# A decoder step on one core: another order of tiles on reused bytes, and four scalings on another engine

## The chip, the core and the metric

The kernel runs on one core of a Trainium2 chip. Five engines work beside each other, each through a queue of its own in order: TensorE (PE in the profile; PEld is its weight load), VectorE (DVE), ScalarE (ACT), GpSimd (POOL) and SyncE (SP), which here issues most DMA transfers. An instruction at the head of a queue that has to wait holds up all that stands behind it. The metric is the device time of one execution in microseconds; lower is better.

## The reference

One layer of a hybrid decoder, for a prompt of 512 tokens and eight samples of four new tokens each that share all weights:

```python
h = rmsnorm(x, w['norm1']) * (1 + sc1) + sh1
bg, cg, xin, q, kc, vc, ks, vs, kw, vw, nsa_g, merge_g = split_columns(h @ w['w_in'])
v, conv_new = short_conv(cg * xin, conv_prev, w['w_conv'], w['b_conv'])
y_a = (bg * v) @ w['w_out_conv']
o_b, nsa_state = attend(qh, gates, kvh(kc, vc), kvh(ks, vs), kvh(kw, vw))
y_b = o_b @ w['w_o_nsa']
x = x + g1 * ((ga * y_a + gb * y_b) @ w['w_out'])
h2 = rmsnorm(x, w['norm2']) * (1 + sc2) + sh2
x = x + g2 * ((jax.nn.silu(h2 @ w['w_gate']) * (h2 @ w['w_up'])) @ w['w_down'])
```

The attention has three branches, each with its own softmax: over compressed blocks, over selected blocks, over a window. The outputs are added with one gate for each head and branch:

```python
s_w = jnp.einsum('bqgrd,bkgd->bgrqk', q, kw).astype(jnp.float32) - sl * w_dist
p_w = jax.nn.softmax(jnp.where(w_valid, s_w, NEG), axis=-1)
o_w = jnp.einsum('bgrqk,bkgd->bqgrd', p_w.astype(vw.dtype), vw)
o = gates[..., 0:1] * o_c + gates[..., 1:2] * o_s + gates[..., 2:3] * o_w
```

The prompt attends to itself; with 512 tokens all its blocks are selected. The samples attend to 1,024 older tokens in a paged cache as well.

## The kernel before

Activations lie feature by feature: 128 partitions, eight slices of features, 544 tokens (32 of the samples, 512 of the prompt). Large products are made of three matmuls each (L247 to L249), with both operands split in a high and a low part: ScalarE copies the high part, VectorE subtracts it. The weights come as slabs of 1 MB through SyncE's queue into a ring of three buffers (L233, tile `raw`).

The stages in order: compressed keys of the samples; input projections; sample attention, in four pairs of samples, with the rest of the projections and the short convolution as filling between its steps; prompt attention; output projections; feed-forward. The change lies at the passage from sample to prompt attention.

**Sample attention** (`rows_gen`, L1116 on) keeps the cache rows in a ring of seven buffers of 8 KB per partition (`sraw`, `wraw`; pool `srp`). Each pair takes four for selected rows (two samples, two halves each) and two for window rows, in turn. For each pair TensorE computes the selected scores, multiplies the selected values (L1166 on `sraw`), then the window scores and the window values (L1166 on `wraw`). There follow a transpose of the remaining probabilities (L1187), the product of these (L1195) and a transpose of the output (L1200).

**Prompt attention** goes through four head groups `g`, and in each through four blocks of 128 queries, `i` = 3, 2, 1, 0. `cmp_probs(g)` makes the compressed probabilities: eight matmuls (L1340), a copy by ScalarE (L1342), four transposes (L1345), then VectorE's operations L1352 to L1360. `unit(g, i)` makes the scores of the two other branches (L1385, L1386, or L1378, L1379 for short blocks). VectorE adds the distance table and finds the row minimum (L1391), ScalarE takes the exponential and the row sum (L1392), VectorE scales by gate over sum (`fac`, L1401). Then TensorE transposes the probabilities (L1416), ScalarE copies them (now and then VectorE, L1333 and L1335), and TensorE multiplies the values (L1410). The eight probability tiles of the first unit, `g` = 0 and `i` = 3, use the output tile `oT` as storage. Between the pieces of the first unit, the last input projections (`for _ in fill`, L247 to L249 on `h`) and the splits of the convolution's output (`split_y`, L380 and L381 on `yin`) are made; behind it come the projections of that output (`oc_gen`) and the modulation products (`mod_slab`, L399).

**What is loaded for it** at its start, all through SyncE's queue: the table `ta` (L1281, 0.32 MB), the queries of the first group (`q_stack`, L1297), its keys, high and low (`k_stack`, L1290), the values of both branches (`vtok`, L1303) and two slabs behind them (L1305). Two tiles for queries and two sets for keys take turns by `g % 2`.

**Where these tiles lie.** The framework gives pools bytes like a stack, from two ends. The row ring is given back before prompt attention starts (`cst2.close()`), and the pool `at1` lies on its bytes. A new tile waits for the last reader of every old tile that it overlaps, and for that alone. Within a pool the tiles lie upwards in the order in which the code makes them. From the sizes (queries 8 KB per partition, high and low keys 4 KB each, values 4 KB for each branch, table 2.5 KB), `at1` begins 14,464 bytes into the ring. In the last pair the ring's seven buffers hold, from below: selected rows of the second sample, second half and first half; of the first sample, second half and first half; window rows of the pair before, no longer read; window rows of the second sample; of the first sample. So the tiles lie now:

| tile | bytes of the ring | what lay there |
|---|---|---|
| first queries `qs0` | 14,464 to 22,656 | selected rows |
| second queries `qs1` | 22,656 to 30,848 | selected rows |
| values `vtok0` | 30,848 to 34,944 | selected rows, free buffer |
| values `vtok1` | 34,944 to 39,040 | free buffer |
| second keys | 39,040 to 47,232 | free buffer, window rows |
| first keys | 47,232 to 55,424 | window rows of both samples |
| table `ta` | 55,424 to 57,984 | window rows of the first sample, and 640 bytes above the ring |

**The order of the queues.** A planner of the framework orders each engine's queue when the program is built: it takes the instructions in program order but lets a later one go ahead of one that, by its own reckoning, still waits. PSUM tiles of the tag `g` (five buffers) serve projections, transposes and half of the scores.

Of the kernel before, what the change touches and what calls it, by code (L numbers as in the profile page):

```python
# [10 lines left out]
F32 = mybir.dt.float32  # L11
F32R = mybir.dt.float32r
I32 = mybir.dt.int32
AF = mybir.ActivationFunctionType
# [7 lines left out]
TP = 512  # L22
# [125 lines left out]
TA_W = 512 + 128  # L148
# [3 lines left out]
def build(tc, a, o):  # L152
    nc = tc.nc
    sync, act, dve, pool, pe = nc.sync, nc.scalar, nc.vector, nc.gpsimd, nc.tensor
    top = ExitStack()

    def mkpool(stack, name, space=None, side="left"):
        if space is DRAM:
            return stack.enter_context(tc.tile_pool(name=name, bufs=1, space=DRAM))
        if space is PSUM:  # L160
            return stack.enter_context(tc.tile_pool(name=name, bufs=1, space=PSUM))
        return stack.enter_context(tc.tile_pool(name=name, bufs=1, side=side, reuse_waits="tile"))
# [9 lines left out]
    def tp_ps(nm):  # L172
        return ps.tile([128, 512], F32, tag="g", bufs=5, name=nm)

    def s_ps(nm):
        return ps.tile([128, 512], F32, tag="sc", bufs=2, name=nm)

    def acc_ps(nm):
        return ps.tile([128, 512], F32, tag="acc", bufs=1, name=nm)
# [3 lines left out]
    def nm(s):  # L183
        uid[0] += 1
        return f"{s}_{uid[0]}"
# [1088 lines left out]
    C = yinf  # L1274
    pst = ExitStack()
    at1 = mkpool(pst, "at1", side="right")
    qs_ = [at1.tile([128, 4, TP], F32R, name=f"qs{j}") for j in range(2)]
    vtok = [at1.tile([128, 4, 256], F32, name=f"vtok{br}") for br in range(2)]
    ks_ = [[at1.tile([128, 2, TP], F32R, name=f"k{n}{j}") for n in "hl"] for j in (1, 0)][::-1]
    ta = at1.tile([128, TA_W], F32, name="ta")  # L1280
    sync.dma_start(ta, a["tab_a"])  # L1281
    t_dist = ta[:, 0:512]
    t_cd = ta[:, 512:640].rearrange("p (i c) -> p i c", i=4)
# [46 lines left out]
    def pev(out, in_):  # L1330
        pcnt[0] += 1
        if pcnt[0] % 6:
            act.activation(out, in_, AF.Copy)  # L1333
        else:
            dve.tensor_copy(out, in_)  # L1335
# [28 lines left out]
    def unit(g, i, ks, qs, pc, beside=lambda r: None):  # L1364

        n = 128 * (i + 1)
        gp, gg = g // 2, g % 2
        sums = at.tile([128, 8], F32, tag="sums", bufs=2, name=nm("sums"))
        nms = at.tile([128, 8], F32, tag="nms", bufs=2, name=nm("nms"))
        P = {}  # L1370
        for r in range(4):
            hs = SLOPES[4 * g + r]
            ql = qs[:, r, 128 * i:128 * i + 128]
            kh, kl = ks
            if 2 * n <= 512:
                sp = s_ps(nm("sp"))[:, 0:2 * n]
                spv = sp.rearrange("p (b x) -> p b x", b=2)
                pe.matmul(sp, lhsT=ql, rhs=kh[:, :, 0:n], start=True, stop=False)  # L1378
                pe.matmul(sp, lhsT=ql, rhs=kl[:, :, 0:n], start=False, stop=True)  # L1379
                sps = [spv[:, 0, :], spv[:, 1, :]]  # L1380
            else:
                sps = []
                for br in range(2):
                    sp = (s_ps if br else lin_ps)(nm("sp"))
                    pe.matmul(sp[:, 0:n], lhsT=ql, rhs=kh[:, br, 0:n], start=True, stop=False)  # L1385
                    pe.matmul(sp[:, 0:n], lhsT=ql, rhs=kl[:, br, 0:n], start=False, stop=True)  # L1386
                    sps.append(sp[:, 0:n])
            for br in range(2):
                c = br * 4 + r
                t = oT[:, br * 4 + r, :] if g == 0 and i == 3 else atp.tile([128, 512 if i % 2 else 384], F32, tag="PX" if i % 2 else "PY", bufs=8, name=nm("P"))  # L1390
                p_ops.append(dve.tensor_tensor_reduce(out=t[:, 0:n], in0=sps[br], in1=t_dist[:, 512 - n:512], scale=-hs, scalar=3e38, op0=ALU.add, op1=ALU.min, accum_out=nms[:, c:c + 1]))  # L1391
                e_ops.append(act.activation(t[:, 0:n], t[:, 0:n], AF.Exp, scale=-1.0, bias=nms[:, c:c + 1], accum_out=sums[:, c:c + 1]))  # L1392
                P[br, r] = t
            beside(r)
        fac = at.tile([128, 8], F32, tag="fac", bufs=2, name=nm("fac"))
        dve.reciprocal(fac, sums)
        dve.tensor_mul(fac.rearrange("p (b r) -> p b r", b=2), fac.rearrange("p (b r) -> p b r", b=2), gtok[:, i, g * 12:(g + 1) * 12].rearrange("p (r b) -> p b r", b=3)[:, 1:3])
        for br in range(2):
            for r in range(4):
                c = br * 4 + r  # L1400
                dve.tensor_scalar_mul(P[br, r][:, 0:n], P[br, r][:, 0:n], fac[:, c:c + 1])  # L1401
        yield
        acc = acc_ps(nm("acc"))
        pend = None
        tp = tp_ps(nm("ctp"))
        pe.transpose(tp[:, 0:128], pc[:, i].rearrange("p r c -> p (r c)"), ident)
        act.activation(pct, tp[:, 0:128], AF.Copy)
        def pv_pair(j, pts_):
            for br in range(2):
                pe.matmul(acc[br * 64:br * 64 + 64, :], lhsT=vtok[br][:, j, g * 64:(g + 1) * 64], rhs=pts_[br], start=(j == 0), stop=False)  # L1410
        for j in range(i + 1):
            pts_ = []
            for br in range(2):
                tp = tp_ps(nm("ptp"))
                for r in range(4):
                    pe.transpose(tp[:, r * 128:(r + 1) * 128], P[br, r][:, 128 * j:128 * j + 128], ident)  # L1416
                ptt = at.tile([128, 512], F32, tag="PT", bufs=4, name=nm("PT"))
                pev(ptt, tp)
                pts_.append(ptt)
            if pend is not None:  # L1420
                pv_pair(*pend)
            pend = (j, pts_)
        pv_pair(*pend)
        for r in (0, 2, 1, 3):
            q = (r // 2) * 64
            pe.matmul(acc[q:q + 64, r * 128:(r + 1) * 128], lhsT=vm[:, g, r, :], rhs=pct, start=False, stop=(r % 2 == 1))
        tmp = at.tile([128, 512], F32, tag="PT", bufs=4, name=nm("otmp"))[0:64]
        act.activation(tmp, acc[64:128, :], AF.Copy)
        dve.tensor_add(oT[gg * 64:gg * 64 + 64, gp * 4:gp * 4 + 4, 128 * i:128 * i + 128], acc[0:64, :].rearrange("p (r q) -> p r q", r=4), tmp.rearrange("p (r q) -> p r q", r=4))
# [5 lines left out]

    first_pc = cmp_probs(0, qst)
    first_unit = unit(0, 3, kst, qst, first_pc, split_y)
    next(first_unit)
    for _ in fill:
# [18 lines left out]
    for g in range(4):  # L1458
        qs, ks = qst, kst
        pc = cmp_probs(g, qs) if g else first_pc  # L1460
        for i in (3, 2, 1, 0):
            u = unit(g, i, ks, qs, pc) if g or i < 3 else first_unit
            if g or i < 3:
                next(u)
            next(ocf, None)
            mod_slab(nslab, mods_ahead.pop(0) if mods_ahead else None)
            nslab += 1
            if prev is not None:
                next(prev, None)
            prev = u  # L1470
            if g < 3 and i == 3:
                qst = q_stack(g + 1)
            if g < 3 and i == 2:
                kst = k_stack(g + 1)
# [27 lines left out]
    for k2 in range(4):  # L1502
        sy = slab("o", k2)
        for kk in range(2):
            k = k2 * 2 + kk
# [406 lines left out]
```

## Time and profile before

| | |
|---|---|
| median of 3 runs | 1240.37 us (1239.27 to 1240.58) |
| the profiled execution | 1242.07 us, of which its span 1240.3 us |
| mean granted TensorE clock | 0.994 |
| instructions | 25,490 |
| HBM read, written | 181.60 MB, 29.11 MB |

The profile is one execution. A row of the timeline gives start, duration, engine, line, operation and tiles, and in brackets how long the engine had been idle and what released it. A row of the windows gives a stretch, its length, the busy time of each engine with the number of instructions, the granted clock, the share of the DMA engines and GB/s. A row of the waits gives who waited for what, the sum, how often, the longest. A row of one tile or line gives the shortest, median and longest duration in ns. Durations of neighbours overlap a little, since an engine starts an instruction before the one ahead has quite ended; a sequence is measured from start to start.

### The profile page before, as it was taken

To read this page: it belongs to the slowest core of one execution; us is meant where nothing else is said; L and a number is where in the kernel's file an instruction comes from. 1 tells how busy PE (TensorE), PEld (TensorE's weight loads), DVE (VectorE), ACT (ScalarE), POOL (GpSimd) and SP (SyncE) were. 2 spreads that over 40 slices of the span, in tenths; PEclk is the share of its full clock that TensorE was granted. 3 is DMA by queue.
4 is the path that set the end of the run, shared out by engine and by line. 5 is a ranking of instruction groups with operands and counts; after the bars stand their busy time and mean duration, and the time that the engine had idled before them with its cause. 6 is when DMAs were issued, how large, how long until landed. Compare 5 with 4: busy or idle time off the path is not lost.

```text
span 1240.3 us, 25490 instructions
## 1 busy us (share of the span) xinstructions
PE 1215.6 (98%) x10254; PEld 1122.1 (90%) x10254; DVE 834.6 (67%) x1853; ACT 624.6 (50%) x1206; POOL 54.3 (4%) x105
## 2 busy tenths in 40 slices
PE   8999999999999999979999999999999999999997
PEld 6999999999999888867767778999999999999997
DVE  4467427687775567666858776667985688666866
ACT  5456435564545433347667666436653255424542
POOL 1000310000000101110000000001000000000000
PEclk9999999999999999989999999999999999999999
DMA  8954244364443998594744325333532433223212
GB/s 285 408 204 168 96 157 154 131 204 157 156 147 131 342 351 296 217 254 154 213 120 138 136 87 209 106 136 101 156 137 99 161 114 136 103 103 136 86 52 73
DMA packets 58920, 205.14 MB, mean 165 GB/s; under 512 B 7208, under 2 KB 13224, under 8 KB 43578
## 3 DMA queue, kind: packets, MB, share of 16 engines
q1 hardware_dynamic: 56898, 199.57, 46.4%
q0 software_dynamic: 1472, 3.56, 1.4%
q8 instruction: 80, 1.31, 0.5%
q10 hardware_dynamic: 432, 0.39, 0.1%
q14 instruction: 38, 0.31, 0.1%
HBM read 181.60 MB, written 29.11 MB: 170 GB/s over the span
## 4 chain that ended last, share of the span: by engine, by line
PE 55%; DVE 2%; ACT 1%; DMA 1%; issue 0%; DVEq 0%; SPq 0%; ACTq 0%
PE lin L247 5%; PE lin L248 5%; PE lin L249 5%; PE wA L247 4%; PE dn L247 4%; PE dn L249 4%; PE dn L248 3%; PE acc L1410 3%; PE wA L248 3%; PE wA L249 3%; PE ptp L1416 3%; PE wC L249 2%; PE wC L248 2%; PE wC L247 2%; PE modp L399 1%; PE sp L1385 1%
## 5 line engine op out<-in xcount | busy, mean ns | idle before, releaser
L247 PE MATMUL lin<-h_h,wh 128*128 128x288 f32 (+1 forms) x416 | 122.3, 294 | 0.0
L248 PE MATMUL lin<-h_l,wh 128*128 128x288 f32 (+1 forms) x416 | 120.2, 289 | 0.0
L249 PE MATMUL lin<-h_h,wl 128*128 128x288 f32 (+1 forms) x416 | 119.7, 288 | 0.0
L242 ACT ACTIVATE wh<-raw 128x1024 fp32r<-128x1024 f32 x62 | 65.5, 1056 | 102.5 <-PE lin L248 38.2
L243 DVE TENSOR_TENSOR wl<-raw,wh 128x1024 fp32r<-128x1024 f32 x62 | 76.0, 1226 | 36.8 <-ACT wh L242 36.0
L247 PE MATMUL dn<-f_hilo,wh 128*128 128x288 f32 (+1 forms) x304 | 88.0, 290 | 0.1
L249 PE MATMUL dn<-f_hilo,wl 128*128 128x288 f32 (+1 forms) x304 | 87.6, 289 | 0.0
L248 PE MATMUL dn<-f_hilo,wh 128*128 128x288 f32 (+1 forms) x304 | 87.2, 287 | 0.0
L247 PEld LDWEIGHTS lin<-h_h,wh 128*128 128x128 f32 x416 | 79.0, 190 | 7.7 <-issue 6.9
L248 PEld LDWEIGHTS lin<-h_l,wh 128*128 128x128 f32 x416 | 78.5, 189 | 0.2
L249 PEld LDWEIGHTS lin<-h_h,wl 128*128 128x128 f32 x416 | 78.1, 188 | 0.1
L1392 ACT ACTIVATE P<-P,nms 128x384 f32<-128x384 f32 (+3 forms) x120 | 65.0, 544 | 23.8 <-DVE nms L1391 23.1
L296 ACT ACTIVATE work<-wA 128x272 f32<-128x272 f32 x111 | 43.8, 395 | 61.7 <-PE wA L249 59.9
L648 PE MATMUL phi<-xh,wph 128*128 128x256 f32 x256 | 72.0, 290 | 1.5 <-ACT xh L630 1.0
L1391 DVE CUSTOM_DVE_ANT_0 P<-sp,ta 128x384 f32<-128x384 f32 (+3 forms) x120 | 52.3, 469 | 31.4 <-PE sp L1379 24.4
L648 PE MATMUL phi<-xl,wph 128*128 128x256 f32 x256 | 70.5, 284 | 0.9 <-DVE xl L631 0.9
L648 PE MATMUL phi<-xh,wpl 128*128 128x256 f32 x256 | 70.2, 283 | 0.0
L381 DVE TENSOR_TENSOR Wl<-ws,Wh 128x1024 fp32r<-128x1024 f32 x37 | 45.3, 1225 | 32.2 <-ACT Wh L380 31.9
L380 ACT ACTIVATE wh<-raw 128x1024 fp32r<-128x1024 f32 (+2 forms) x41 | 42.2, 1030 | 31.5 <-PE dn L248 13.1
L380 ACT ACTIVATE wh<-ws 128x1024 fp32r<-128x1024 f32 x37 | 39.3, 1061 | 37.0 <-PE wB L248 23.6
L247 PEld LDWEIGHTS dn<-f_hilo,wh 128*128 128x128 f32 x304 | 57.1, 188 | 0.6 <-ACT f_hilo L380 0.3
L249 PEld LDWEIGHTS dn<-f_hilo,wl 128*128 128x128 f32 x304 | 57.3, 189 | 0.1
(506 smaller groups left out, 4125.6 us busy)
## 6 DMA issues: line engine op xcount, KB each, us to landing
raw<-in_wt SPq DMA_DIRECT2D x97, 1024.0 KB, 5.3
sraw<-in_cache_sel SPq DMA_DIRECT2D x64, 256.0 KB, 5.0
gt<-in_cache_cmp SPq DMA_DIRECT2D x56, 256.0 KB, 5.2
wraw<-in_cache_winT SPq DMA_DIRECT2D x8, 1024.0 KB, 9.5
out_new_win_sample<-in_cache_win SPq DMA_DIRECT2D x8, 512.0 KB, 5.8
out_new_win_sample<-in_cache_win SPq DMA_DIRECT2D x8, 504.0 KB
out_kvT<-kvT SPq DMA_DIRECT2D x12, 272.0 KB, 2.1
raw<-in_wt SPq DMA_DIRECT2D x4, 768.0 KB, 4.3
```

The lines of the kernel that those rows point to most:

```text
L242: act.activation(oh, view, AF.Copy)
L243: dve.tensor_sub(ol, view, oh.bitcast(F32))
L247: pe.matmul(p, lhsT=wh[:, k, :], rhs=xh, start=start, stop=False, **kw)
L248: pe.matmul(p, lhsT=wh[:, k, :], rhs=xl, start=False, stop=False, **kw)
L249: pe.matmul(p, lhsT=wl[:, k, :], rhs=xh, start=False, stop=stop, **kw)
L296: o_.snap_ops.append(act.activation(t, p, AF.Copy))
L380: act.activation(hi, src, AF.Copy)
L381: return dve.tensor_sub(lo, src, hi.bitcast(F32))
L648: pe.matmul(po[:, s * 256:s * 256 + 256], lhsT=w, rhs=m, start=(n_ == 0), stop=(n_ == len(ops) - 1))
L1391: p_ops.append(dve.tensor_tensor_reduce(out=t[:, 0:n], in0=sps[br], in1=t_dist[:, 512 - n:512], scale=-hs, scalar=3e38, op0=ALU.add, op1=A ...
L1392: e_ops.append(act.activation(t[:, 0:n], t[:, 0:n], AF.Exp, scale=-1.0, bias=nms[:, c:c + 1], accum_out=sums[:, c:c + 1]))
L1410: pe.matmul(acc[br * 64:br * 64 + 64, :], lhsT=vtok[br][:, j, g * 64:(g + 1) * 64], rhs=pts_[br], start=(j == 0), stop=False)
```

## The change

The tiles of `at1` are made in another order, and the second four of the eight scalings in the very first unit go to ScalarE.

```diff
-    qs_ = [at1.tile([128, 4, TP], F32R, name=f"qs{j}") for j in range(2)]
+    k_tiles = lambda j: [at1.tile([128, 2, TP], F32R, name=f"k{n}{j}") for n in "hl"]
+    qs_ = [at1.tile([128, 4, TP], F32R, name="qs0")]
+    ks_ = [k_tiles(0)]
+    ta = at1.tile([128, TA_W], F32, name="ta")
     vtok = [at1.tile([128, 4, 256], F32, name=f"vtok{br}") for br in range(2)]
-    ks_ = [[at1.tile([128, 2, TP], F32R, name=f"k{n}{j}") for n in "hl"] for j in (1, 0)][::-1]
-    ta = at1.tile([128, TA_W], F32, name="ta")
+    qs_.append(at1.tile([128, 4, TP], F32R, name="qs1"))
+    ks_.append(k_tiles(1))
     sync.dma_start(ta, a["tab_a"])
...
-                dve.tensor_scalar_mul(P[br, r][:, 0:n], P[br, r][:, 0:n], fac[:, c:c + 1])
+                if g == 0 and i == 3 and br:
+                    act.activation(P[br, r][:, 0:n], P[br, r][:, 0:n], AF.Copy, scale=fac[:, c:c + 1])
+                else:
+                    dve.tensor_scalar_mul(P[br, r][:, 0:n], P[br, r][:, 0:n], fac[:, c:c + 1])
```

The sizes stay, so the pool covers the same bytes. By the same arithmetic the tiles then lie:

| tile | bytes of the ring | what lay there |
|---|---|---|
| first queries `qs0` | 14,464 to 22,656 | selected rows |
| first keys | 22,656 to 30,848 | selected rows |
| table `ta` | 30,848 to 33,408 | selected rows, free buffer |
| values `vtok0` | 33,408 to 37,504 | free buffer |
| values `vtok1` | 37,504 to 41,600 | free buffer, 640 bytes of window rows |
| second queries `qs1` | 41,600 to 49,792 | window rows of both samples |
| second keys | 49,792 to 57,984 | window rows of the first sample, and 640 bytes above the ring |

The transfers and their place in the program stay as they are. The `if` holds for `g` = 0, `i` = 3 and the second branch (`br` = 1), so for four instructions of 128x512 in the whole program.

## The prediction

> **What bounds the kernel now.** I read the page first: engine shares, slices, the chain that ended last. Then who waited for whom on TensorE, then windows and the timeline of the one stretch with a long wait.
>
> ```profile
> PE 1215.6 (98%) x10254; PEld 1122.1 (90%) x10254; DVE 834.6 (67%) x1853; ACT 624.6 (50%) x1206; POOL 54.3 (4%) x105
> engine line waited for: us in total, times, longest us
> PE cpt L1340 <- DMA qs<-q_dr0l: 6.1, 1, 6.1
> ...
> PE lin L247 <- DVE nms L1391: 1.3, 1, 1.3
> ...
> PE sp L1385 <- DMA kh<-k_dr0h: 0.3, 1, 0.3
> ```
>
> TensorE is busy for 98% of the span, so time is won only where it stands still or runs slowly. In its waits over the whole run the longest is 6.1 us: the first compressed scores of the prompt's attention (L1340) wait for the query load. A wait of 1.3 for the first score sums of the second unit follows a little later. Both lie in the stretch that the change edits. What TensorE and SyncE do there:
>
> ```profile
> 511.48 1.95 PE L1166 MATMUL sacc<-sraw,pts 128*32 128x128 f32 x64
> 522.59 1.08 PE L1166 MATMUL sacc<-wraw,pts 128*32 128x128 f32 x32
> 526.27 0.33 PE L1200 MATMUL ot<-ident,ob 128*128 128x128 f32 x1 [0.40 <-ACT ob L1197]
> 532.67 1.94 PE L1340 MATMUL cpt<-qs,kcd 128*32 128x512 f32 x8 [6.07 <-DMA qs<-q_dr0l]
> 534.92 0.77 PE L1385 MATMUL sp<-kh,qs 128*128 128x512 f32 x1 [0.32 <-DMA kh<-k_dr0h]
> 535.49 1.06 PE L1345 MATMUL cps<-ident,cpT 128*128 128x128 f32 x4
> 536.20 2.48 PE L1385 MATMUL sp<-kh,qs 128*128 128x512 f32 x5
> 538.48 0.41 PE L247 MATMUL lin<-h_h,wh 128*128 128x256 f32 x1
> SPq L1281 <- PE ptx L1187: 20.9, 1, 20.9
> 501.50 1.48 SPq L233 DMA_DIRECT2D raw<-in_wt  x2
> 523.70 0.33 SPq L1281 DMA_DIRECT2D ta<-in_tab_a  x1
> 524.64 0.59 SPq L1297 DMA_DIRECT2D qs<-q_dr0l  x1
> 526.55 1.29 SPq L1290 DMA_DIRECT2D kl<-k_dr0l  x2
> 527.89 1.07 SPq L1303 DMA_DIRECT2D vtok<-v_dr  x2
> 530.28 2.65 SPq L233 DMA_DIRECT2D raw<-in_wt  x2
> 535.91 1.28 SPq L1290 DMA_DIRECT2D kh<-k_dr0h  x2
> SPq L1290 <- DMA kl<-k_dr0l: 1.0, 2, 0.6
> 513.50:523.70 10.20, 9.59 (x102) 8.15 (x94) 7.86 (x19) 3.07 (x7) 1.04 (x2) 1.00 0.01 2
> 528.00:529.00 1.00, 0.00 (x0) 0.00 (x0) 0.00 (x0) 0.00 (x0) 0.00 (x0) 0.75 1.08 246
> 532.70:538.50 5.80, 5.48 (x19) 3.16 (x20) 1.85 (x3) 0.60 (x1) 0.00 (x0) 0.50 1.04 314
> ```
>
> SyncE's queue stands for 20.9 us, from the slab loads at 501.50 to 523.70, at the table load (L1281). The table lies on the last pair's first window rows, so it may only land when TensorE has multiplied the window values (L1166 on wraw, 522.59 + 1.08 = 523.67); the profile names the transpose behind it. Queries and keys stand behind the table in that queue, and the keys lie on window rows themselves. In the 10.2 us of this standing the transfer engines move nothing (DMA share 0.01). Then everything is loaded at once, while TensorE finishes its sample work at 526.60 and has nothing until 532.67. Meanwhile its granted clock falls and stays at half through the first scores (0.50).
>
> **The change, part by part.** *The order of the tiles.* Worked out from the sizes in the code, the queries stay where they are (rows of two selected parts); the first keys move onto selected rows, the table onto selected rows and a window buffer of the pair before; the first values follow on that old buffer, the second values reach 640 bytes into the last pair's second window rows. Second queries and keys take the last pair's window rows. So table, queries and keys now wait for the selected values, 511.48 + 1.95 = 513.43, instead of 523.67. Nothing is added or removed: the same loads in the same sizes, 10.2 us earlier, into a stretch where DMA does nothing.
>
> When do they land? Before, the first scores began 8.97 us after the table's issue (523.70 to 532.67), with everything else in flight too; 513.43 + 8.97 gives 522.4. The loads of the second keys at 535.91 waited for the landing of the first low keys (the row under it), so the latter were there when the second of the two was issued, 536.55 at the latest: 12.85 after the table, so 526.3. TensorE asks for the queries at 526.60 and for the low keys one us later. Both margins are positive, 4.2 and over 1 us. The new wait that the change brings, second values on window rows, stands in SyncE's queue until 523.67; behind it are the two slabs of L1305 and the second queries and keys. Before, those slabs went at 530.28, so they go earlier as well.
>
> What TensorE gains: the idle 6.07, the wait for the keys 0.32, and the slow clock. For the last I take the same work where the clock is full, the next head group:
>
> ```profile
> 594.57 1.07 PE L1340 MATMUL cpt<-qs,kcd 128*32 128x512 f32 x8
> 595.57 0.50 PE L1385 MATMUL sp<-kh,qs 128*128 128x512 f32 x1
> 596.61 0.60 PE L1345 MATMUL cps<-ident,cpT 128*128 128x128 f32 x4
> 596.96 0.48 PE L1385 MATMUL sp<-kh,qs 128*128 128x512 f32 x1
> ```
>
> There eight compressed-score matmuls take 1.00 from start to start, four score matmuls 1.04 (0.26 each), four transposes 0.35. The first unit runs eight, six and four between 532.67 and 538.48: 1.00 + 1.56 + 0.35 = 2.91 at full clock, against 5.81 - 0.32 = 5.49 now. The slow clock costs 2.58. After the change I expect no gap over the 0.40 that stands before L1200, so none of it.
>
> [...]
>
> *Half the first scaling on ScalarE.* Of the eight scalings of the first unit (L1401) the last four leave VectorE.
>
> ```profile
> 540.46 0.69 DVE L1391 CUSTOM_DVE_ANT_0 oT<-sp,ta 128x512 f32<-128x512 f32 x1 [1.02 <-PE sp L1386]
> 553.92 4.20 DVE L1401 TENSOR_SCALAR oT<-oT,fac 128x512 f32<-128x512 f32 x7
> 555.89 1.15 DVE L1401 TENSOR_SCALAR oT<-oT,fac 128x512 f32<-128x512 f32 x2
> 558.03 0.54 DVE L1391 CUSTOM_DVE_ANT_0 P<-sp,ta 128x384 f32<-128x384 f32 x1
> 558.64 0.39 PE L247 MATMUL lin<-yin_hi,wh 128*128 128x256 f32 x1 [1.29 <-DVE nms L1391]
> 563.65 1.91 PE L1416 MATMUL ptp<-ident,oT 128*128 128x128 f32 x16
> 553.03 1.05 ACT L242 ACTIVATE wh<-raw 128x1024 fp32r<-128x1024 f32 x1
> 558.62 0.62 ACT L1392 ACTIVATE P<-P,nms 128x384 f32<-128x384 f32 x1 [3.49 <-DVE nms L1391]
> 562.83 0.60 ACT L1392 ACTIVATE P<-P,nms 128x384 f32<-128x384 f32 x1
> L907 ACT ACTIVATE qh<-work,hd x8: 723/724/727, 237.5 to 274.5; 128x512 fp32r<-128x512 f32 x8
> ```
>
> On VectorE the four take 2.14 (555.89 to 558.03). TensorE stands 1.29 until the next unit's first sum, which is queued right behind them. ScalarE idles 3.49 there, and its nearest form, a copy scaled per partition on 128x512 (L907), takes 0.72: four take 2.9.
>
> Does the 1.29 go? The softmax chain of the first unit starts at 540.46 (L1391), 1.02 of which VectorE waited for TensorE; so it was through with the compressed scores at 539.44, 3.95 after the transposes of L1345 began, 3.49 with these at full clock (0.60 for 1.06). From L1340 to L1345 it is 2.04 in the later group. So the chain starts at 526.60 + 2.04 + 3.49 = 532.1, 8.3 earlier. VectorE comes to the second unit at 558.03 - 8.3 - 2.14 = 547.6 and is done with its first sum 0.54 later, 548.1. TensorE wants that at 557.35 (558.64 less the wait) less 6.07 + 0.32 + 2.58, 548.4. So the 1.29 goes. ScalarE ends the split of L242 at 554.08 - 8.3 = 545.8, the scalings at 548.7, then the eight exponentials that now last from 558.62 to 563.43: 553.5. TensorE needs it for the transposes' copies soon after 563.65 - 10.26 = 553.4. That fits with nothing to spare, and ScalarE is late next.
>
> Sum: 6.07 + 0.32 + 2.58 + 1.29 = 10.26. I count 10.2, with 0.1 for ScalarE. From there on TensorE's own work sets the pace:
>
> ```profile
> 600.00:700.00 100.00, 100.00 (x864) 1.00 0.45 142
> ```
>
> There TensorE is 100% busy with a DMA share under one half, so what is won before is kept. The profiled execution took 1242.07 (span 1240.3 and 1.8 around it) and would take 1231.9. The median, 1240.37, lies 1.7 below it; less 10.2 it is **1230.2**.
>
> **Rivals.** *ScalarE becomes the bound* of the first two units. For: it has no slack, and the four scalings may be queued ahead of the weight split or behind the exponentials. If each takes up to the 1.05 of the 1024-column pass of L242 instead of 0.72, that is 1.3, and with a bad order up to 2: 1231.5 to 1232.2. Against: the scalings fill an idle 3.49.
>
> *The loads are not hidden, or only in part*: the planner, which orders every queue at build time, puts the second values, with their wait until 523.67, ahead of queries or keys, or they land slowly. If wholly so, only the 1.29 is won: 1239.1. Twice the landing time (18 us after 513.43) leaves a gap of 4.8 and a cold start, a gain of some 3: 1237. Against: the values' loads come last in the program and in the trace (527.89); the transfer engines are free.
>
> *Slower: the first scores move ahead in TensorE's queue.* The planner does move work past waiting work: the slab load at 501.50 stands behind the table in the program. If it believes the queries present at, say, 513.5, the eight matmuls of L1340 stop TensorE until 522.4, 9.0 us where it now loses 6.07 + 0.32, at half clock after two of them (2.6 as now), and the sample's last work follows behind: 2.6 more, 1243.0. It decides from a place in the queue before about 513.5; by 520 the stop is 2.4 and most of the gain stays. Against: the accumulators of L1340 come from the same five-buffer ring as the transposes before it, and the trace takes these in program order, L1200 first, L1340 behind.
>
> **How the numbers follow.** The forecast with its small errors (1228.5 to 1231): 0.64. ScalarE the bound (1231 to 1232.5): 0.16. Loads hidden in part or not at all (1234 to 1239.5): 0.09, half of it within 0.2%, which is 2.5 us and about what a measurement of this kernel can tell from no change. Slower (1241 to 1245): 0.05. More than forecast, because the chain starts on VectorE before the compressed scores and fills the 0.40 before L1200: 1226.5 to 1228.5, 0.06. Range 1227.5 to 1233.5, which leaves out the third and fourth case and half of the last. Faster 0.90, within 0.2% 0.05, slower 0.05.
>
> **What would show it.** Right: the table's issue near 513.5 and a DMA share well above 0.01 up to 523.7; no wait of L1340 or L1385 for a DMA; clock 1.00 through 540; the transposes of L1416 ten us earlier; ScalarE with four copies of about 0.7 on oT. Wrong: SyncE still at the table at 520, L1340 with a wait anywhere, TensorE waiting for ScalarE in L1416 or L1410, or a later stretch where it is less than 99% busy.

## The result and the profile after

| | before | after |
|---|---|---|
| median of 6 runs each | 1240.47 us (1239.27 to 1240.95) | 1231.35 us (1230.64 to 1233.15) |
| ratio, 95% interval | | 0.993 (0.9917 to 0.9942) |
| the profiled execution | 1242.07, span 1240.3 | 1232.06, span 1230.3 |
| mean granted TensorE clock | 0.994 | 0.998 |

The median fell by 9.1 us. The forecast was 1230.2, with a range of 1227.5 to 1233.5; for the profiled execution 1231.9, where 1232.06 was measured.

SyncE's queue after the change, from the timeline (start, duration, engine, line, tiles). The changed code stands three lines further down, and six lines from the scalings on.

```profile
513.17 0.33 SPq L1284 DMA_DIRECT2D ta<-in_tab_a  x1
514.04 0.51 SPq L1300 DMA_DIRECT2D qs<-q_dr0h  x1
515.24 2.34 SPq L1293 DMA_DIRECT2D kh<-k_dr0h  x2
517.63 1.24 SPq L1293 DMA_DIRECT2D kl<-k_dr0l  x2
518.91 5.72 SPq L1306 DMA_DIRECT2D vtok<-v_dr  x2
```

The table goes out at 513.17 instead of 523.70, with queries and keys right behind it. The two value loads now hold the place in which the table used to wait: 5.72 with the second one's wait for the window rows. The same stretch in the windows (length, busy time of PE, PEld, DVE, ACT and POOL, granted clock, DMA share, GB/s):

```profile
513.50:523.70 10.20, 9.60 (x108) 8.24 (x104) 8.43 (x19) 3.64 (x7) 0.47 (x1) 1.00 0.92 210
528.00:540.00 12.00, 11.71 (x81) 10.46 (x78) 10.24 (x26) 7.98 (x19) 1.72 (x2) 1.00 1.03 301
```

A DMA share of 0.92 stands where it was 0.01, and TensorE does as much in it as before (9.60 for 9.59); from the last selected value products to L1200 it takes 14.78 (512.06 to 526.84), 14.79 before (511.48 to 526.27): the loads cost the sample work nothing. In the second row the clock is 1.00 where it was 0.50 up to 538.5. TensorE in that place, timeline:

```profile
526.84 0.33 PE L1200 MATMUL ot<-ident,ob 128*128 128x128 f32 x1 [0.40 <-ACT ob L1197]
527.10 1.07 PE L1343 MATMUL cpt<-qs,kcd 128*32 128x512 f32 x8
528.10 0.50 PE L1388 MATMUL sp<-kh,qs 128*128 128x512 f32 x1
528.88 0.66 PE L1348 MATMUL cps<-ident,cpT 128*128 128x128 f32 x4 [0.29 <-ACT cpT L1345]
529.29 1.52 PE L1388 MATMUL sp<-kh,qs 128*128 128x512 f32 x5
530.66 0.28 PE L247 MATMUL lin<-h_h,wh 128*128 128x256 f32 x1
```

The first compressed scores (now L1343) follow L1200 by 0.26 instead of 6.40. A small wait has appeared, 0.29 for ScalarE's copy `cpT`, of which more below. VectorE, ScalarE and, in the last row, TensorE, from the same timeline:

```profile
532.51 0.69 DVE L1394 CUSTOM_DVE_ANT_0 oT<-sp,ta 128x512 f32<-128x512 f32 x1
547.68 0.56 DVE L1394 CUSTOM_DVE_ANT_0 P<-sp,ta 128x384 f32<-128x384 f32 x1 [0.45 <-PE sp L1389]
544.80 2.56 ACT L1405 ACTIVATE oT<-oT,fac 128x512 f32<-128x512 f32 x4
548.28 0.62 ACT L1395 ACTIVATE P<-P,nms 128x384 f32<-128x384 f32 x1 [0.49 <-DVE nms L1394]
552.50 0.60 ACT L1395 ACTIVATE P<-P,nms 128x384 f32<-128x384 f32 x1
554.80 1.36 PE L1422 MATMUL ptp<-ident,oT 128*128 128x128 f32 x11
```

The four scalings on ScalarE take 2.56 together, 0.64 for each. VectorE reaches the second unit (547.68) and even waits 0.45 there for TensorE; before, TensorE waited 1.29 for VectorE. ScalarE has finished the second unit's exponentials at 553.10, before TensorE begins the transposes.

**Where the 10 us of the two profiled executions lie.** The output adds of VectorE make good milestones. The second of them, in the timeline of before and of after:

```profile
585.54 0.68 DVE L1429 TENSOR_TENSOR oT<-acc,otmp 64x512 f32<-64x512 f32 x1
```

```profile
576.01 0.68 DVE L1435 TENSOR_TENSOR oT<-acc,otmp 64x512 f32<-64x512 f32 x1
```

And all sixteen, in the rows of the tile (durations in ns, then the start of the first and the last), before and after:

```profile
L1429 DVE TENSOR_TENSOR oT<-acc,otmp x16: 672/682/685, 573.0 to 756.2; 64x512 f32<-64x512 f32 x16
```

```profile
L1435 DVE TENSOR_TENSOR oT<-acc,otmp x16: 677/683/685, 563.9 to 746.2; 64x512 f32<-64x512 f32 x16
```

From L1200 (526.27; after 526.84) to the second add, 59.27 before and 49.17 after: 10.10 won. From the second to the last add, 170.64 and 170.17: 0.5 won, a gain that the prediction doesn't have. From the last add to the end of the span, 484.1 and 484.1: nothing is given back. These legs are used for all kernels below, since the time up to L1200, which the change doesn't touch, differs between executions (525.7 to 528.7 in the eleven traces).

### The profile page after: what moved, and what is told of

It reads as the page before. It is cut to its first block, busy times and chain, and to the rows that moved or that the text cites. A ratio compares the mean times of both kernels' runs of the same rounds, so it can differ in the third digit from the quotient of the medians.

```text
span 1230.3 us, 25493 instructions
## 1 busy us (share of the span) xinstructions
PE 1213.0 (99%) x10254; PEld 1120.3 (91%) x10254; DVE 832.0 (68%) x1849; ACT 627.1 (51%) x1210; POOL 54.8 (4%) x105
## 4 chain that ended last, share of the span: by engine, by line
PE 56%; DVE 1%; ACT 0%; issue 0%; DVEq 0%; ACTq 0%
PE lin L248 5%; PE lin L247 5%; PE lin L249 5%; PE wA L247 4%; PE dn L247 4%; PE dn L249 4%; PE dn L248 3%; PE acc L1416 3%; PE wA L248 3%; PE wA L249 3%; PE ptp L1422 3%; PE wC L249 2%; PE wC L248 2%; PE wC L247 2%; PE modp L399 1%; PE sp L1388 1%
## 5 line engine op out<-in xcount | busy, mean ns | idle before, releaser
L380 ACT ACTIVATE Wh<-ws 128x1024 fp32r<-128x1024 f32 x37 | 39.2, 1060 | 35.7 <-PE wC L248 28.6
```

The costliest lines, as they stand in the source:

```text
L380: act.activation(hi, src, AF.Copy)
```

## The experiments

Theory: the loads' place in SyncE's queue was the cause of the gap, and each term (idle, keys, half clock, first sum) adds up. Rivals: the gain comes from the scalings alone; the order of tiles matters because of the keys' bytes and not the table's; the half clock costs nothing by itself; ScalarE sets the pace after the change.

| kernel | median us | ratio to before, 95% | L1200 to 2nd add | 2nd to last add |
|---|---|---|---|---|
| before | 1240.47 | | 59.27 | 170.6 |
| after | 1231.35 | 0.993 (0.9917 to 0.9942) | 49.17 | 170.2 |
| whole change again | 1231.59 | 0.9923 (0.9909 to 0.9936) | 49.2 | 170.2 |
| order alone | 1232.69 | 0.9933 (0.9919 to 0.9946) | 50.8 | 170.2 |
| scalings alone | 1239.64 | 0.9989 (0.998 to 0.9998) | 56.41 | 170.6 |
| gap filled | 1244.79 | 1.0021 (1.001 to 1.0033) | 61.4 | 170.6 |
| gap filled, same order | 1239.12 | 0.9983 (0.9974 to 0.9993) | 58.40 | 170.7 |
| keys late | 1234.24 | 0.9945 (0.9932 to 0.9959) | 50.17 | 170.1 |
| all on ScalarE | 1233.88 | 0.9946 (0.9932 to 0.9959) | 50.4 | 170.2 |
| before again, one run | 1240.61 | | 57.64 | 170.7 |
| values above second keys, one run | 1241.95 | | 58.95 | 170.1 |

**The whole change again**, unaltered, beside its halves on one chip.

> The whole change once more, beside its two halves. My theory: the sum of both, 10.2 us less than before (1230.3); rival: less than the sum, since ScalarE is late next, 9 us less (1231.4).

1231.59 (1230.91 to 1231.99), and both legs within 0.1 of the first execution's. The 9.7 less than before on that chip lies between the 10.2 of the theory and the 9 of the rival and doesn't decide between them.

**The order of the tiles alone.** The loop over the scalings is that of before:

```diff
-                if g == 0 and i == 3 and br:
-                    act.activation(P[br, r][:, 0:n], P[br, r][:, 0:n], AF.Copy, scale=fac[:, c:c + 1])
-                else:
-                    dve.tensor_scalar_mul(P[br, r][:, 0:n], P[br, r][:, 0:n], fac[:, c:c + 1])
+                dve.tensor_scalar_mul(P[br, r][:, 0:n], P[br, r][:, 0:n], fac[:, c:c + 1])
```

> The new order of tiles with all eight scalings on VectorE. My theory: the table issues near 513, no wait of the first compressed scores, clock 1.00 through 540, so 6.07 + 0.32 + 2.58 = 8.97 us less than before, near 1231.5; the wait of 1.3 for the first sum of the second unit stays in the profile. Rival (the scalings make the gain possible, since the chain of the first unit sets the pace): a gain of 6 us or less, with new waits of TensorE for ScalarE or VectorE that add up to 3. Second rival (the scalings bring nothing): the same time as the whole change within 0.3 us, and no wait for that sum.

1232.69, 8.6 below the 1241.26 of before on that chip (0.9933): nearly the whole gain. All five queues have the instructions in the order of before, so nothing but the bytes acts. The wait for the second unit's first sum stays, in TensorE's waits:

```profile
PE lin L247 <- DVE nms L1394: 1.3, 1, 1.3
```

**The scalings alone.** The other half of the diff, the tiles as before.

> The old order of tiles with four of the first unit's scalings on ScalarE. My theory: the wait of 1.29 for the first sum of the second unit goes, all else stays as before (wait of 6.1 for the queries, half clock), so 1.3 us less, near 1239.2. Rival (ScalarE has no slack, so the wait moves to it): no gain, 1240.5, and a wait of TensorE for ScalarE in the transposes or value products of the first unit of 1 us or more.

1239.64, a ratio of 0.9989 (0.998 to 0.9998). The two halves add up within their intervals: by the medians of that chip 8.6 and 1.6, together 10.2, against 9.7 for the whole. The 1.3 is gone from TensorE's waits, and the gap stands:

```profile
534.22 1.94 PE L1340 MATMUL cpt<-qs,kcd 128*32 128x512 f32 x8 [5.70 <-DMA qs<-q_dr0l]
536.46 0.77 PE L1385 MATMUL sp<-kh,qs 128*128 128x512 f32 x1 [0.30 <-DMA kh<-k_dr0h]
539.20 0.29 PE L247 MATMUL lin<-h_h,wh 128*128 128x256 f32 x1
```

The edit does a little more than move four instructions. The planner reckons with them, draws a few scores forward in TensorE's queue and one key load in SyncE's, and puts the scalings ahead of a weight split on ScalarE, here and in the changed kernel alike.

**Keys late.** Before, with the table alone made first in `at1`. Table and queries then lie on selected rows; the first keys are still on window rows.

```diff
     at1 = mkpool(pst, "at1", side="right")
+    ta = at1.tile([128, TA_W], F32, name="ta")
     qs_ = [at1.tile([128, 4, TP], F32R, name=f"qs{j}") for j in range(2)]
...
-    ta = at1.tile([128, TA_W], F32, name="ta")
```

> The old order of tiles with the table alone moved ahead, so that table and first queries lie on selected rows and the first keys still on window rows; all queues keep their order. My theory: table and queries issue near 513, the first compressed scores wait for nothing; the keys issue near 524 with little else in flight and land 4 to 5 us later, so the first scores wait about 1 us, the clock stays at 1.00, and the gain is 1 us smaller than with the new order alone. Rival (keys need the 11 us they took before): a wait of 7 us at L1385 and a gain of 2 us or less.

1234.24 (0.9945). Its timeline:

```profile
514.74 0.33 SPq L1281 DMA_DIRECT2D ta<-in_tab_a  x1
524.98 1.37 SPq L1290 DMA_DIRECT2D kh<-k_dr0h  x2
527.82 1.06 PE L1340 MATMUL cpt<-qs,kcd 128*32 128x512 f32 x8
530.11 0.47 PE L1385 MATMUL sp<-kh,qs 128*128 128x512 f32 x1 [1.23 <-DMA kh<-k_dr0h]
```

The queries, on selected rows as before, now come in time only because nothing stands in front of them in the queue. So the table at its head was the main block, and the keys' bytes leave a wait of 1.23. A gap of 1.23 left the clock at full speed here: behind it, the four transposes of L1345 take 0.60 (530.42), where they took 1.06 at half clock before, and the eight matmuls ahead of it take 1.06 for 1.94.

In time the 1.23 doesn't show. The median is 1.5 above that of order alone, on another chip; but in the two profiled executions, which stand at these medians, L1200 starts 1.75 later in keys late (527.56 against 525.81), and its first leg is 0.6 shorter than that of order alone. What makes up for the wait is the first sum: TensorE doesn't wait for it here, though all eight scalings are on VectorE. GpSimd works beside them: it sets a tile `vm` to zero and fills it with four copies. Its rows of before, and the last seven scalings and GpSimd's first row in keys late:

```profile
554.62 1.06 POOL L1450 MEMSET vm<- 128x1024 f32 x1 [0.64 <-DMA gb_dr<-gb]
555.75 2.08 POOL L1453 COPY vm<-vcp 32x256 f32<-32x256 f32 x4
```

```profile
547.45 2.85 DVE L1401 TENSOR_SCALAR oT<-oT,fac 128x512 f32<-128x512 f32 x7
549.51 1.68 POOL L1450 MEMSET vm<- 128x1024 f32 x1 [1.99 <-PE sp L1386]
```

The last seven scalings take 2.85 in keys late and 4.20 before (the row of 553.92 in the prediction). Before, the one beside the MEMSET takes 1.26 and the four beside the copies 0.61 or 0.62, where the others take 0.48 or 0.49. The difference of 1.35 is about the wait of 1.29. The gap filled with the same order, below, fits with that: its eight scalings go from 481 to 1259 ns with a median of 485, those of before from 481 to 1259 with a median of 612, and the wait is 1.00 there. So the first sum is late because VectorE's scalings run slower while GpSimd fills `vm`. In the changed kernel the MEMSET starts at 548.47, behind VectorE's share of the scalings. Whether moving GpSimd's work alone would do as well was not tried.

**The gap filled.** Before, with matmuls on an identity put in front of the first compressed scores, so that TensorE waits as long but is not idle. First with six on the shared five-buffer ring:

```diff
+    wake(6)
```

> The kernel before, with six matmuls of 128x512 on a constant (their result is not read) between the last output transpose of the samples and the first compressed scores: TensorE works about 5 us in the gap, and the loads stay as they were. My theory: the clock stays at 1.00 or nearly so, and the 2.58 us of the slow clock go while the rest of the gap stays: near 1237.9, up to 0.6 more because the planner now puts the transposes directly behind the scores. [...] Rival (the slow stretch costs nothing, since the softmax chain behind it sets the pace): 1240.5.

1244.79 (1.0021), slower: a miss. The clock stayed up in the gap, as expected (1.00 in every us from 525 to 545), but the planner, which reckons with the new matmuls and their ring, moved a weight split on ScalarE behind; TensorE's waits show its price:

```profile
PE lin L247 <- ACT wh L242: 2.9, 1, 2.9
PE cps L1345 <- ACT cpT L1342: 0.7, 1, 0.7
```

The mean granted clock of this execution is 0.993, below the 0.994 of before, so the clock was down elsewhere instead. This kernel tells nothing of the clock alone. The second try takes five matmuls on a bank that no neighbour uses, and every queue keeps its order:

```diff
-    def wake(n):
+    def wake(n, ring=tp_ps):
...
-        p = tp_ps(nm("wake"))
+        p = ring(nm("wake"))
...
+    wake(5, acc_ps)
```

> The filled gap again, now with five matmuls on the accumulator bank, so that every queue keeps the order of the kernel before (the first try had shifted a ring of five, and the planner had put a weight split later, at 2.9 us). My theory: the clock stays at 1.00 through 541, L1340 takes about 1.0 for its eight, and what is gained is what the half clock cost, 2.6 in the profiled run of before, 1.3 to 2.6 over executions since the half clock lasted 10.2 us there and 6.8 in the run of the scalings alone: median 1.3 to 2.6 less than before. Rival (the slow stretch costs nothing): no difference.

1239.12 (0.9983; 0.9974 to 0.9993): by the ratio 2.1 us less, 0.9 to 3.2, though not one load comes earlier. Its profiled execution was the slowest of its eleven (1243.59), and there the clock didn't stay up through 541 as expected; timeline and windows:

```profile
534.82 1.07 PE L1340 MATMUL cpt<-qs,kcd 128*32 128x512 f32 x8 [1.48 <-DMA qs<-q_dr0l]
537.01 0.47 PE L1385 MATMUL sp<-kh,qs 128*128 128x512 f32 x1 [1.13 <-DMA kh<-k_dr0h]
540.25 0.41 PE L247 MATMUL lin<-h_h,wh 128*128 128x256 f32 x1
```

```profile
534.00:537.40 3.40, 1.46 (x10) 0.54 (x11) 0.00 (x0) 0.60 (x1) 0.00 (x0) 0.99 1.03 236
537.40:540.80 3.40, 3.40 (x13) 2.92 (x12) 2.34 (x4) 0.00 (x0) 0.00 (x0) 0.50 1.03 349
```

The first scores run at full clock (1.07 for the eight), the wait for the keys is longer instead (1.13 for 0.32), and then 3.4 us go by at half speed (0.50) all the same. Six of the eleven executions had a mean granted clock of 0.998, as high as any of the changed kernel, and took 1237.9 to 1239.2; those of before on that chip had 0.992 to 0.995 and a median of 1240.91. That the slow clock has a price of its own is shown by the ratio and by these clocks; its size by the rows in the next section.

**All eight scalings on ScalarE.** The changed kernel with `if g == 0 and i == 3:`, to see whether ScalarE is late next.

> The whole change with all eight of the first unit's scalings on ScalarE. My theory (ScalarE has almost no slack after the change): four more of 0.64 make it 2.1 later at the second unit's exponentials, after the 0.5 it idles there now, and TensorE waits 1 to 1.5 us for it in the transposes or value products: 1 to 1.5 slower than the whole change. Rival (there is cover): the same within 0.3.

1233.88 (0.9946); the first leg is 1.2 longer than with four.

```profile
543.65 5.00 ACT L1405 ACTIVATE oT<-oT,fac 128x512 f32<-128x512 f32 x8
```

Eight take 5.00 on ScalarE, four 2.56. TensorE's waits list nothing that the changed kernel lacks, so they don't show where the loss lies, and the planner's order differs a little from that of the changed kernel; so the 1.2 is no clean price of ScalarE. The ratios' intervals overlap (0.9932 to 0.9959 against 0.9917 to 0.9942): that eight are worse than four is likely, no more.

**Before again**, one more execution, for the spread of the terms.

> A second look at the kernel before. If the half clock begins and ends on a grid of 3.41 us, as the two runs with 10.2 and 6.8 us suggest, it lasts 6.8 or 10.2 us again; the wait for the queries is 5.5 to 6.5, and the time from L1200 to the last output add is 227 to 230 us. Rival (its length follows the work): any other length.

```profile
531.99 1.94 PE L1340 MATMUL cpt<-qs,kcd 128*32 128x512 f32 x8 [5.25 <-DMA qs<-q_dr0l]
534.22 0.77 PE L1385 MATMUL sp<-kh,qs 128*128 128x512 f32 x1 [0.29 <-DMA kh<-k_dr0h]
537.43 0.28 PE L247 MATMUL lin<-h_h,wh 128*128 128x256 f32 x1
557.16 0.39 PE L247 MATMUL lin<-yin_hi,wh 128*128 128x256 f32 x1 [1.01 <-DVE nms L1391]
```

Same kernel, other sizes: the wait for the queries 5.25 (6.07), below the 5.5 to 6.5 expected, the first sum 1.01 (1.29), the stretch from the first scores to the next projection 5.44 (5.81). The granted clock was 0.80 in the two us from 529, 0.50 from 531 to 537 and 1.00 behind, so the half clock lasted 6.8 us, one of the two lengths expected.

**The values above the second keys.** This asks for the 0.5 at the far end. ScalarE's first split of the attention output, in the timelines of before and of after, and TensorE's wait of before, which the waits of after lack:

```profile
754.49 0.42 ACT L380 ACTIVATE o_hi<-o_s 128x256 fp32r<-128x256 f32 x1 [1.16 <-PE acc L1410]
```

```profile
744.49 0.42 ACT L380 ACTIVATE o_hi<-o_s 128x256 fp32r<-128x256 f32 x1 [0.67 <-PE acc L1416]
```

```profile
PE lin L247 <- ACT o_hi L380: 0.6, 1, 0.6
```

`o_hi` is a tile of the stage behind, on bytes that `at1` gives back, and the split has nothing to do with the last value product except by these bytes. The test leaves the first keys and the table where they were and lifts the values by 4 KB, with the low half of the second keys below them:

```diff
+    kl1 = at1.tile([128, 2, TP], F32R, name="kl1")
     vtok = [at1.tile([128, 4, 256], F32, name=f"vtok{br}") for br in range(2)]
-    ks_ = [[at1.tile([128, 2, TP], F32R, name=f"k{n}{j}") for n in "hl"] for j in (1, 0)][::-1]
+    kh1 = at1.tile([128, 2, TP], F32R, name="kh1")
+    ks_ = [[at1.tile([128, 2, TP], F32R, name=f"k{n}0") for n in "hl"], [kh1, kl1]]
```

> Before, with one tile moved: the low half of the second keys (4 KB) now lies below the two value tiles, so the values lie 4 KB higher; first keys and table stay on their bytes. All five queues keep the order of before. Question: what ends the 0.6 us that TensorE waits, at the start of the output projections, for ScalarE's first split (L380 on o_s), a wait that the changed kernel and the kernel with only the table moved do not have. Theory: the split's output tile lies on the bytes of the first values in before and so waits for their last matmul (L1410); with the values higher it waits for less. Then ScalarE's idle before that split falls from 1.16 to about 0.67, TensorE's wait of 0.6 goes, and from the second to the last output add it takes 170.2 instead of 170.7; the waits for queries (5 to 6), keys (0.3) and first sum (1.0 to 1.3) and the half clock stay as in before. Rival: the wait went because everything comes ten us earlier against the weight loads; then it stays at 0.6 and the leg at 170.7 here, since nothing comes earlier.

```profile
753.89 0.42 ACT L380 ACTIVATE o_hi<-o_s 128x256 fp32r<-128x256 f32 x1 [0.67 <-PE acc L1412]
532.64 1.94 PE L1342 MATMUL cpt<-qs,kcd 128*32 128x512 f32 x8 [5.82 <-DMA qs<-q_dr0l]
534.77 0.77 PE L1387 MATMUL sp<-kh,qs 128*128 128x512 f32 x1 [0.20 <-DMA kh<-k_dr0h]
538.33 0.41 PE L247 MATMUL lin<-h_h,wh 128*128 128x256 f32 x1
```

The gap of before stands (5.82), nothing comes earlier, and the split's wait falls to 0.67; TensorE's 0.6 is gone, and the second leg takes 170.1. So the 0.5 is a matter of bytes too. In the change it was the table, 2.5 KB below the values, that lifted them out of the way. No version tried beats the changed kernel.

## Why the prediction was right, point by point

**The order and its margins: right.** The issue at 513.17 (predicted 513.43), a DMA share of 0.92, no wait of L1343 or L1388 for a load in TensorE's waits, clock 1.00 through 540: these signs came as named. The softmax chain started at 532.51, predicted 532.1 for an execution whose L1200 is 0.57 earlier. The transposes L1416, forecast ten us earlier, begin 8.85 earlier (554.80 for 563.65), 9.4 if measured from L1200.

**The half clock: the step was right, its size holds for one execution.** With the same subtraction as in the prediction (first scores to next projection, less the wait for the keys, less 2.91) the slow clock cost:

| execution | wait for queries | slow clock |
|---|---|---|
| before | 6.07 | 5.81 - 0.32 - 2.91 = 2.58 |
| values above second keys | 5.82 | 5.69 - 0.20 - 2.91 = 2.58 |
| before again | 5.25 | 5.44 - 0.29 - 2.91 = 2.24 |
| scalings alone | 5.70 | 4.98 - 0.30 - 2.91 = 1.77 |
| gap filled, same order | 1.48 | 5.43 - 1.13 - 2.91 = 1.39 |

The two rows of 2.58 and the last row leave out another 0.1 to 0.3, since their slow stretch reaches into the projections, whose first matmuls take 0.41 where later ones take 0.28. The granted clock shows why the sizes differ: from the top of the table, it was at half for 10.2, 10.2, 6.8, 6.8 and 3.4 us. Before, scalings alone, and values above second keys, in the windows (the other two are above):

```profile
528.50:538.70 10.20, 5.71 (x20) 3.42 (x21) 2.05 (x3) 0.60 (x1) 0.00 (x0) 0.50 1.02 277
```

```profile
531.30:538.10 6.80, 3.58 (x14) 1.75 (x15) 0.00 (x0) 0.60 (x1) 0.00 (x0) 0.50 1.01 222
```

```profile
528.00:529.00 1.00, 0.00 (x0) 0.00 (x0) 0.00 (x0) 0.00 (x0) 0.00 (x0) 0.81 1.00 197
529.00:538.00 9.00, 5.16 (x18) 2.85 (x19) 1.50 (x3) 0.60 (x1) 0.00 (x0) 0.50 1.01 267
538.00:540.00 2.00, 2.00 (x15) 1.90 (x14) 1.26 (x2) 0.63 (x1) 0.00 (x0) 0.79 1.03 424
```

These are three, three, two, two and one times 3.4. The clock records of the traces of before and after give it finer: before, 522.24 us at full clock, 10.24 at half and 696.32 at full, which are 153, 3 and 204 times 3.413; after, 1218.56 us at full clock, 357 times. So in the executions of the table the slow clock came in whole steps of 3.4 us; what sets when it falls and for how many steps was not tested. For this gap the steps cost between 1.77 and 2.58, and my 2.58 is the upper end.

**The first sum: right in size, its cause only half seen.** The wait of 1.29 is gone; between order alone and the whole change the first leg differs by 1.6, of which this wait is 1.35. The prediction priced the four scalings on VectorE at 2.14, which is what they take beside GpSimd's work; in keys late, four take 1.6 from start to start. VectorE reached the second unit at 547.2 (547.68 less its wait), 546.7 on the clock of the execution predicted from, where 547.6 was predicted: most of the difference is the scaling of 1.26, which takes 0.48 after the change. That moving four scalings ends the wait is shown by scalings alone; that they have to move for it is not, since keys late lacks the wait with all eight on VectorE.

**ScalarE: right that it isn't the bound.** One scaling takes 0.72, as taken from L907, but neighbours overlap, so the four take 2.56 and not 2.9. Its exponentials end at 553.10, 552.5 on the clock of the execution predicted from (predicted 553.5), and TensorE doesn't wait for it there. The 0.1 was not needed. With eight scalings there is likely a loss, so half was enough.

**Two things the steps left out, which nearly cancel.** First, the gap had hidden a wait: TensorE makes the first score and then needs ScalarE's copy `cpT`. From that score to the transposes it is now 0.78 from start to start, where a score takes 0.26: 0.52 lost, of which the waits list 0.29. The term 2.91 was taken from a group where nothing is waited for. Secondly, the 0.5 at the output projections, since the rearranged bytes are passed on once more. For the order alone that is 8.97 less 0.52, 8.45, where the first leg gave 8.5 (59.27 less 50.8). The other 0.3 of the first leg comes with the scalings (1.6 for 1.29), whose planner's order moves scores as well; it was not traced further.

**The median: 1.15 above the forecast.** For the profiled executions the forecast was 0.2 off, in part by luck: the first leg won 10.10, the output projections another 0.5, and the work up to L1200 happened to end 0.57 later. The step that failed is the last one: the saving of an execution of 1242.07 was taken from a median 1.7 lower. In before again, which took 1240.61, the same four terms sum to 5.25 + 0.29 + 2.24 + 1.01 = 8.79; taken from the median of 1240.47 that gives 1231.7, against 1231.35 measured. So the mis-sized terms are the wait for the queries and the slow clock, which vary by 0.8 each between executions. These are few traces, and how the terms are spread over all runs stays open.

**The rivals.** Loads hidden in part: what it would look like is shown by keys late (1.23 left). ScalarE the bound: only with eight scalings, if at all. Slower, by first scores moved ahead in TensorE's queue: didn't arise, as the planner kept every queue's order in order alone; it wasn't forced in a run, so its price stays untested.

## What to carry to other kernels

In a queue that works in order, a load whose bytes come free late holds back all loads behind it, whatever bytes they go to (here the table held back queries and keys for 10.2 us): give the bytes that come free first to what is issued and needed first. Look at both ends of a rearranged pool, since the next stage's tiles wait for the last readers on the same bytes. When an instruction takes longer than its kind in one place, look at what another engine does just then (here 1.26 for a scaling beside GpSimd's MEMSET, 0.48 without), before putting the wait behind it down to the amount of work. And when a gap's cost is taken from one profiled execution, subtract it from that execution, and look how long its clock was at half: here 3.4, 6.8 or 10.2 us.

## What the hardware showed that was not expected

The clock fell although TensorE had worked for part of the 3.4 us before. Before, the 3.41 us up to the fall:

```profile
525.09:528.50 3.41, 1.11 (x13) 0.49 (x11) 0.75 (x4) 0.58 (x2) 0.00 (x0) 1.00 1.00 267
```

TensorE was busy for 1.11 of 3.41 there, and in the gap filled with the same order, in the row from 534.00 shown above, for 1.46 of 3.40; the clock of the next 3.4 us was 0.50 in both. In that filled gap TensorE's waits were 1.48 and 1.13, so no stretch of 3.4 us was idle there. Keys late, with a single wait of 1.23, kept its clock. Before kept it around its wait of 1.29, where TensorE was busy for 2.13 of 3.42:

```profile
555.81:559.23 3.42, 2.13 (x14) 1.81 (x14) 3.42 (x10) 0.61 (x2) 1.86 (x4) 1.00 0.04 14
```

From 538.7 on its clock stayed at 1.00 to the end of the work. How much idling it takes for the clock to fall is not shown by these few stretches.

There is also a slow stretch far ahead of the change, in some executions and not in others. 22.7 us into the span, scalings alone and then before:

```profile
22.70:26.10 3.40, 3.40 (x19) 3.40 (x18) 2.26 (x5) 1.16 (x3) 0.00 (x0) 0.50 0.83 243
```

```profile
22.70:26.10 3.40, 3.40 (x31) 3.40 (x30) 2.09 (x6) 1.65 (x4) 0.00 (x0) 1.00 0.77 231
```

Nineteen matmuls instead of 31 go through in the same time. Keys late has the slow stretch as well (clock 0.53 from 22.50 to 25.90). In these two, L1200 starts at 528.19 and 527.56. The changed kernel has 1.00 there like before, and the whole change again and order alone have a mean of 1.00 over the first 100 us, where scalings alone has 0.98; in these four L1200 starts at 525.8 to 526.8. Up to there the code is the same in all kernels. So a difference of one us or two between two executions of these kernels needs no cause in the stage that was changed.
